# First stage of a hybrid attention and recurrence step: modulation products issued four at a time instead of two

## The chip, the core and the metric

One Trainium2 chip, one of its cores. The time is device microseconds of one execution of the whole program; lower is better. A profile is one execution taken by the hardware profiler; its span runs from the first to the last instruction. The engines are TensorE (PE; its weight loads are PEld), VectorE (DVE), ScalarE (ACT), GpSimd (POOL) and SyncE (SP), which issues all transfers of this kernel from one queue in order.

## What is computed

One layer for 512 tokens of a noisy sample and 128 tokens of context, 2048 features, shared weights. Each group of tokens has its own conditioning vector, from which a large product makes six vectors of shift, scale and gate:

```python
def _adaln(cond, w_mod, b_mod):
    m = jax.nn.silu(cond) @ w_mod + b_mod        # 2048 x 12288
    return jnp.split(m[:, None, :], 6, axis=-1)

sh1, sc1, g1, sh2, sc2, g2 = _adaln(c, p["w_mod"], p["b_mod"])
proj = (x * (1 + sc1) + sh1) @ p["w_in"]
...  # attention and recurrence on parts of proj
x = _post_norm(x, g1, _merge(att, rw, p), p["ln1_g"], p["ln1_b"])
x = _post_norm(x, g2, _swiglu(x * (1 + sc2) + sh2, p), p["ln2_g"], p["ln2_b"])
```

Nothing of the input projection can start on a feature before that feature's shift and scale are there. All is in 32-bit floating point; the large products are made of three products of split operands (high and low part).

## The kernel before

Activations lie transposed: 16 row tiles of 128 features by 640 tokens. The modulation weights are cut into 24 chunks of 512 output columns; chunks 0 to 3 give the shift and 4 to 7 the scale that the input projection needs. These eight are computed first, in the order 0, 4, 1, 5, 2, 6, 3, 7, so that the shift and scale of a group of four row tiles come together (`GROUPS`, L58; `first_mods`, L428). Below, "first chunk" to "eighth chunk" means this order. The other 16 chunks (`wmod_ahead`, L336) come later, with one transfer of 1 MB and four products at a time from a single buffer.

A chunk is 16 products (`wmod_chunk`, L344): the stationary operand is 32 columns of `cs`, the activated conditioning (two columns are real), and the moving operand 512 columns of weights. Product number kt goes to the strip `32 * (kt % 4)` of partitions of the output in PSUM, so four consecutive products use four different strips. After 16 products VectorE copies the result out (`ev`), four tiny products with `sel` add the four strips, and VectorE adds the bias to `mod`. After the second chunk of a group the four row tiles are loaded (`x`), modulated (`h`) and split into a high and a low part (`xh`, `xl`) by VectorE and ScalarE.

`wmod_first` (L326) yields the moving operands of a chunk. Each transfer of 512 KB brings two of the 16 (m = 2); its buffers are `N_W` = 6, shared by tag with later wide tiles. It yields the two products of a transfer and then a number, `W_HOP`.

`first_tiles` (L468) is the first part of the input projection: for each group of four row tiles it does nine output tiles: one (`f` = 0) into the accumulator `ps0`, seven as partial sums in two halves of 320 tokens each (12 products per half, into `m`, then added to `part` by VectorE or copied by ScalarE), and one (`f` = 1) into `ps1`. Their weights are loaded by `load_raw` (L256) in 256 KB transfers into three `raw` buffers and split by ScalarE (`whi`) and VectorE (`wlo`).

What sets TensorE's order is a planner that runs while the program is built (`Jobs`, L126). Each job is a generator. A yielded number says how many microseconds, on the planner's own clock, until that job may go on; the planner always advances the ready job of lowest rank. Ranks: recurrence 0, its side work 1, modulation 2 (`first_mods`, then the other 16 chunks), attention 3, projection 4. A product of 32 columns by 512 costs 0.21 us on this clock. TensorE keeps the order in which the jobs issued; the other engines are ordered by a scheduler, and each instruction waits for its own operands and buffers. When the last group is through its tile `f` = 4, the recurrence begins (`rwkv`, L954): the keys are stored, loaded, squared (`kk`) and reduced by its first product on TensorE.

Of the kernel before, what the change touches and what calls it, by code (L numbers as in the profile page):

```python
# [57 lines left out]
GROUPS = ((0, 4), (4, 4), (8, 4), (12, 4))  # L58
N_PART = 7
TURN = 0.5  # L60
W_HOP = 1.0
M_HOP = 4.9
RANK_R = 0
RANK_S = 1
# [95 lines left out]
def step_kernel(ctx: ExitStack, tc: tile.TileContext, a: dict, o: dict, upto: int = 99, npairs: int = NPAIR, dbg=None):  # L160
# [24 lines left out]
    def rtile(name, n, tag, bufs, dtype=F32):  # L185
        return rp.tile([P, n], dtype, tag=tag, name=nm(name), bufs=bufs)
# [139 lines left out]
    def wmod_first(n, c0, w):  # L326

        m = 1024 // w
        for k in range(0, KT, m):
            raw = rtile("wm", 2 * NT, "w", N_W)[:, :1024].rearrange("p (k c) -> p k c", k=m)  # L330
            DMA.dma_start(out=raw, in_=a["w_mod"][n, k: k + m, :, c0: c0 + w].rearrange("k p c -> p k c"))
            for j in range(m):
                yield raw[:, j]
            yield W_HOP

    def wmod_ahead(n):  # L336
        for k in range(0, KT, 4):
# [90 lines left out]
    def first_mods():  # L428
        for k0, nk in GROUPS:
            n, c0 = divmod(k0 * P, 512)  # L430
            for q in (n, 4 + n):
                yield from wmod_chunk(q, wmod_first(q, c0, nk * P), c0, nk * P)
            for kt in range(k0, k0 + nk):
                x, h = slot("x"), edge("h")
                DMA.dma_start(out=x, in_=a["xT"][kt])
                h1.append(modulate(x, h, hslot, 0, 1, kt))
# [1626 lines left out]
```

## Time and profile before

| | us |
|---|---|
| median of 3 runs (3465.1 to 3469.4) | 3466.15 |
| span of the profiled execution | 3458.1 |
| first products with modulation weights | from 8.2 |
| last of the 128 products of the first eight chunks begins at | 171.6 |
| first product of the recurrence | 231.8 |

The profiled execution's own time is not shown apart from its span; the median stands 8.05 us above it. A row of a timeline gives start, duration, engine, line of the program, operation, tile written and tiles read, columns and sizes, and in brackets how long the engine had been idle and what ended it. One product in 32-bit precision with the modulation weights is recorded as two matmuls, so "x4" are two products and "x8" are four.

### The profile page before, as it was taken

To read this page: it belongs to the slowest core of one execution; us is meant where nothing else is said; L and a number is where in the kernel's file an instruction comes from. 1 tells how busy PE (TensorE), PEld (TensorE's weight loads), DVE (VectorE), ACT (ScalarE), POOL (GpSimd) and SP (SyncE) were. 2 spreads that over 40 slices of the span, in tenths; PEclk is the share of its full clock that TensorE was granted. 3 is DMA by queue.
4 is the path that set the end of the run, shared out by engine and by line. 5 is a ranking of instruction groups with operands and counts; after the bars stand their busy time and mean duration, and the time that the engine had idled before them with its cause. 6 is when DMAs were issued, how large, how long until landed. Compare 5 with 4: busy or idle time off the path is not lost.

```text
span 3458.1 us, 70966 instructions
## 1 busy us (share of the span) xinstructions
PE 3254.0 (94%) x27682; PEld 2972.3 (86%) x27682; DVE 2499.6 (72%) x4478; ACT 1449.3 (42%) x3031; POOL 999.1 (29%) x1034
## 2 busy tenths in 40 slices
PE   7988988999999789999979999999999999999998
PEld 4677766777887678989979999999999999999997
DVE  1356766776776666467688988888887778899677
ACT  1144443443444444445453444444444444333234
POOL 0022222222222122102174544444443332222124
PEclk9999999999999799999989999999999999999998
DMA  8754444444221211076534443444343357888643
GB/s 300 246 177 136 147 145 139 158 157 144 78 62 56 73 31 40 29 252 185 154 110 138 165 130 122 145 134 129 125 142 116 118 186 282 298 285 288 222 140 120
DMA packets 284528, 527.71 MB, mean 153 GB/s; under 512 B 30432, under 2 KB 66720, under 8 KB 284192
## 3 DMA queue, kind: packets, MB, share of 16 engines
q1 hardware_dynamic: 284192, 523.18, 46.1%
q8 instruction: 217, 3.56, 0.4%
q14 instruction: 119, 0.97, 0.1%
HBM read 428.99 MB, written 92.44 MB: 151 GB/s over the span
## 4 chain that ended last, share of the span: by engine, by line
PE 58%; DVE 6%; ACT 2%; issue 2%; DMA 1%; POOL 1%; SPq 0%; ACTq 0%; DVEq 0%; POOLq 0%
PE b L114 50%; PE acc L114 4%; PE m L114 2%; DVE z L228 1%; DVE ql L228 1%; POOL z L228 1%; PE x L114 1%; ACT z L240 0%; PE acc L118 0%; DVE smx L1165 0%; DVE pr L228 0%; ACT P L1166 0%; DVE ip L228 0%; DVE raw L228 0%; DMA raw<-in_w_down_dram 0%
## 5 line engine op out<-in xcount | busy, mean ns | idle before, releaser
L228 DVE TENSOR_TENSOR ql<-raw,qh 128x512 fp32r<-128x512 f32 (+1 forms) x1064 | 887.8, 849 | 260.4 <-ACT qh L1303 247.1
L1303 ACT CAST qh<-raw 128x512 fp32r<-128x512 f32 (+1 forms) x1064 | 633.3, 610 | 830.6 <-PE b L114 647.2
L114 PE MATMUL b<-t,qh 128*128 128x320 f32 x2816 | 622.8, 310 | 8.5 <-ACT qh L1303 7.4
L228 POOL TENSOR_TENSOR raw<-raw,raw 128x512 f32<-128x512 f32 x240 | 354.4, 1477 | 804.4 <-DVE ql L228 546.2
L114 PE MATMUL b<-op,qh 128*128 128x320 f32 x2560 | 553.2, 311 | 1.9 <-ACT qh L1303 1.1
L114 PEld LDWEIGHTS b<-t,qh 128*128 128x128 f32 x2816 | 472.6, 189 | 9.7 <-ACT qh L1303 8.1
L114 PE MATMUL b<-p,qh 128*128 128x320 f32 x2112 | 468.9, 311 | 0.0
L114 PE MATMUL b<-t,ql 128*128 128x320 f32 x1408 | 436.1, 310 | 5.6 <-DVE ql L228 5.5
L114 PEld LDWEIGHTS b<-op,qh 128*128 128x128 f32 x2560 | 425.9, 189 | 4.4 <-ACT qh L1303 2.7
L114 PE MATMUL b<-op,ql 128*128 128x320 f32 x1280 | 379.0, 311 | 5.4 <-DVE ql L228 5.3
L114 PEld LDWEIGHTS b<-p,qh 128*128 128x128 f32 x2112 | 356.0, 189 | 0.3
L114 PE MATMUL b<-p,ql 128*128 128x320 f32 x1056 | 329.0, 312 | 6.9 <-DVE ql L228 6.9
L114 PEld LDWEIGHTS b<-t,ql 128*128 128x128 f32 x1408 | 265.0, 188 | 7.8 <-DVE ql L228 7.7
L114 PEld LDWEIGHTS b<-op,ql 128*128 128x128 f32 x1280 | 236.7, 189 | 8.3 <-DVE ql L228 7.9
L114 PE MATMUL b<-mh,qh 128*128 128x320 f32 x1024 | 230.4, 314 | 6.6 <-ACT qh L1303 6.6
L114 PE MATMUL acc<-xh,whi 128*128 128x320 f32 x928 | 230.3, 330 | 3.5 <-ACT P L1166 2.5
L114 PE MATMUL acc<-xl,whi 128*128 128x320 f32 x928 | 232.9, 333 | 0.0
L114 PE MATMUL acc<-xh,wlo 128*128 128x320 f32 x928 | 231.8, 332 | 0.0
L114 PEld LDWEIGHTS b<-p,ql 128*128 128x128 f32 x1056 | 199.8, 189 | 9.6 <-DVE ql L228 9.6
L228 DVE TENSOR_TENSOR raw<-raw,raw 128x512 f32<-128x512 f32 x240 | 185.4, 780 | 12.5 <-POOL raw L228 9.4
L265 ACT CAST whi<-raw 128x512 fp32r<-128x512 f32 (+1 forms) x156 | 94.9, 609 | 226.4 <-PE acc L114 138.9
L114 PEld LDWEIGHTS b<-mh,qh 128*128 128x128 f32 x1024 | 174.5, 191 | 8.3 <-ACT qh L1303 7.8
(330 smaller groups left out, 5654.5 us busy)
## 6 DMA issues: line engine op xcount, KB each, us to landing
wm<-in_w_mod_dram SPq DMA_DIRECT2D x64, 1024.0 KB, 5.3
raw<-in_w_gate_dram SPq DMA_DIRECT2D x188, 256.0 KB, 2.7
raw<-in_w_up_dram SPq DMA_DIRECT2D x188, 256.0 KB, 2.9
op<-hd SPq DMA_DIRECT2D x136, 320.0 KB, 5.4
raw<-in_w_in_dram SPq DMA_DIRECT2D x132, 256.0 KB, 2.7
wm<-in_w_mod_dram SPq DMA_DIRECT2D x64, 512.0 KB, 6.0
raw<-in_w_out_dram SPq DMA_DIRECT2D x128, 256.0 KB, 3.0
raw<-in_w_down_dram SPq DMA_DIRECT2D x128, 256.0 KB, 5.4
```

The source lines that it names most:

```text
L114: self.eng.matmul(out, lhsT, rhs, start=start, stop=stop)
L228: eng.tensor_tensor(out=out, in0=x, in1=y, op=op)
L265: A.copy(hi, r)
L1303: A.copy(hi, x)
```

## The change

`wmod_first` now starts transfers until it holds four operands, so two transfers of 512 KB; then it yields `W_HOP` first and the four products after it. `W_HOP` goes from 1.0 to 2.4. Transfers, buffers and products are the same ones. The wait of each product for its transfer stays with that product.

```diff
-W_HOP = 1.0
+W_HOP = 2.4
...
     def wmod_first(n, c0, w):
 
         m = 1024 // w
+        held = []
         for k in range(0, KT, m):
             raw = rtile("wm", 2 * NT, "w", N_W)[:, :1024].rearrange("p (k c) -> p k c", k=m)
             DMA.dma_start(out=raw, in_=a["w_mod"][n, k: k + m, :, c0: c0 + w].rearrange("k p c -> p k c"))
-            for j in range(m):
-                yield raw[:, j]
-            yield W_HOP
+            held += [raw[:, j] for j in range(m)]
+            if len(held) >= 4:
+                yield W_HOP
+                yield from held
+                held = []
```

How this moves instructions is seen at three places. The first is TensorE's order in the third chunk (output `x_295`), where the first projection products (`acc_154`, tile `f` = 0) begin. A row "x2" is here two products. Before:

```order
L114 MATMUL x_295<-wm_304,cs 32x512 x2
L114 MATMUL x_295<-wm_308,cs 32x512 x2
L114 MATMUL acc_154<-xh_264,whi_176 128x320 x2
L114 MATMUL acc_154<-xl_265,whi_176 128x320 x2
L114 MATMUL x_295<-wm_322,cs 32x512 x2
L114 MATMUL acc_154<-xh_264,wlo_177 128x320 x2
L114 MATMUL acc_154<-xh_273,whi_176 128x320 x2
L114 MATMUL acc_154<-xl_274,whi_176 128x320 x2
L114 MATMUL acc_154<-xh_273,wlo_177 128x320 x2
L114 MATMUL x_295<-wm_334,cs 32x512 x2
```

And of the change:

```order
L114 MATMUL x_295<-wm_296,cs 32x512 x2
L114 MATMUL x_295<-wm_298,cs 32x512 x2
L114 MATMUL acc_154<-xh_264,whi_176 128x320 x2
L114 MATMUL x_295<-wm_304,cs 32x512 x2
L114 MATMUL x_295<-wm_306,cs 32x512 x2
L114 MATMUL acc_154<-xl_265,whi_176 128x320 x2
L114 MATMUL acc_154<-xh_264,wlo_177 128x320 x2
L114 MATMUL acc_154<-xh_273,whi_176 128x320 x2
L114 MATMUL acc_154<-xl_274,whi_176 128x320 x2
L114 MATMUL acc_154<-xh_273,wlo_177 128x320 x2
```

Where one row of modulation products stood between four projection rows, two now stand between ten. The second place is TensorE's order in the fifth chunk (`x_681`), at the end of the first group of row tiles: `acc_155` is its last tile, `acc_154` the first tile of the second group. Before:

```order
L114 MATMUL x_681<-wm_724,cs 32x512 x2
L114 MATMUL x_681<-wm_728,cs 32x512 x2
L114 MATMUL x_681<-wm_732,cs 32x512 x2
L114 MATMUL x_681<-wm_736,cs 32x512 x2
L114 MATMUL acc_154<-xh_650,whi_686 128x320 x2
L114 MATMUL acc_154<-xl_651,whi_686 128x320 x2
L114 MATMUL x_681<-wm_750,cs 32x512 x2
```

And of the change:

```order
L114 MATMUL acc_155<-xh_291,wlo_606 128x320 x2
L114 MATMUL x_681<-wm_714,cs 32x512 x2
L114 MATMUL x_681<-wm_716,cs 32x512 x2
L114 MATMUL x_681<-wm_728,cs 32x512 x2
L114 MATMUL x_681<-wm_730,cs 32x512 x2
L114 MATMUL acc_154<-xh_650,whi_686 128x320 x2
...
L114 MATMUL acc_154<-xl_669,whi_686 128x320 x2
L114 MATMUL acc_154<-xh_668,wlo_687 128x320 x2
L114 MATMUL x_681<-wm_736,cs 32x512 x2
L114 MATMUL x_681<-wm_738,cs 32x512 x2
```

Two quads follow each other directly there, as four pairs did, and the last one comes nine projection rows later instead of two. The third place is SP's queue for the same transfers (`wm` modulation weights, `raw` projection weights, `x` row tiles). Before:

```order
L435 DMA x_1002<-in_xT_dram 128x640
L331 DMA wm_736<-in_w_mod_dram 128x2x512
L258 DMA raw_791<-in_w_in_dram 128x512
L331 DMA wm_750<-in_w_mod_dram 128x2x512
L435 DMA x_1011<-in_xT_dram 128x640
```

And of the change:

```order
L438 DMA x_1027<-in_xT_dram 128x640
L258 DMA raw_780<-in_w_in_dram 128x512
L438 DMA x_1036<-in_xT_dram 128x640
L438 DMA x_1045<-in_xT_dram 128x640
L332 DMA wm_736<-in_w_mod_dram 128x2x512
L332 DMA wm_738<-in_w_mod_dram 128x2x512
L438 DMA x_1054<-in_xT_dram 128x640
```

The last two modulation transfers of the chunk now stand side by side, behind one projection weight and two row tiles.

## The prediction

> **What bounds the kernel now.** I read the page's busy line first, then the first stage by stretches, then the single rows on TensorE.
>
> ```profile
> span 3458.1 us, 70966 instructions
> PE 3254.0 (94%) x27682; PEld 2972.3 (86%) x27682; DVE 2499.6 (72%) x4478; ACT 1449.3 (42%) x3031; POOL 999.1 (29%) x1034
> ```
>
> TensorE is busy for 94% of the span; nothing else is near it. The change lies in the first 5% or so, so the share of the whole says little. The next view is busy time by stretches, with TensorE's clock, the share of the DMA engines and GB/s at the right.
>
> ```profile
> 20.00:41.00 21.00, 16.19 (x60) 4.57 (x64) 1.88 (x5) 0.00 (x0) 0.00 (x0) 0.70 1.05 389
> 60.00:80.00 20.00, 20.00 (x110) 12.78 (x109) 2.77 (x4) 5.05 (x11) 0.00 (x0) 1.00 0.64 198
> 80.00:100.00 20.00, 18.54 (x109) 11.86 (x108) 8.73 (x17) 6.17 (x11) 0.00 (x0) 1.00 0.82 268
> 100.00:120.00 20.00, 19.86 (x114) 13.61 (x114) 4.90 (x9) 1.85 (x3) 0.00 (x0) 1.00 0.91 329
> 41.00:231.80 190.80, 179.49 (x1068) 128.15 (x1062) 75.06 (x143) 50.33 (x95) 7.91 (x26) 1.00 0.69 227
> ```
>
> The reader is to see two regimes. Up to 41 us the DMA engines are full (share 1.05, 389 GB/s) and TensorE takes each transfer as it lands. From 41 us to 231.8 us, where the recurrence's first product starts, TensorE is busy for 179.5 of 190.8 us at full clock, and the DMA engines for 0.69 of the time. So the first regime is set by bytes, the second by what TensorE must issue. What TensorE waited for between 41 and 200 us is little, and only 1.8 us of it is for a modulation transfer:
>
> ```profile
> PE x L114 <- DMA wm<-in_w_mod_dram: 1.8, 2, 1.5
> PE x L114 <- DVE ev L356: 0.8, 1, 0.8
> PE x L114 <- DVE mod L237: 0.3, 1, 0.3
> PE x L114 <- DVE mod L228: 0.3, 1, 0.3
> ```
>
> **The price of an interruption.** First a pair of modulation products (one row "x4" is two products, each recorded twice) between the half tiles of the input projection, then four of them, which the trace already has from the later chunks:
>
> ```profile
> 66.11 0.30 PE L114 MATMUL m<-xh,wlo 128*128 128x320 f32 x1
> 66.34 1.05 PE L114 MATMUL x<-wm,cs 128*32 128x512 f32 x4
> 67.32 0.41 PE L114 MATMUL m<-xh,whi 128*128 128x320 f32 x1
> 67.57 0.31 PE L114 MATMUL m<-xl,whi 128*128 128x320 f32 x1
> ...
> 69.04 0.31 PE L114 MATMUL m<-xh,wlo 128*128 128x320 f32 x1
> 69.28 1.05 PE L114 MATMUL x<-wm,cs 128*32 128x512 f32 x4
> ```
> ```profile
> 207.41 0.31 PE L114 MATMUL m<-xh,wlo 128*128 128x320 f32 x1
> 207.65 1.07 PE L114 MATMUL x<-wm,cs 128*32 128x512 f32 x8
> 208.64 0.41 PE L114 MATMUL m<-xh,whi 128*128 128x320 f32 x1
> 208.89 0.31 PE L114 MATMUL m<-xl,whi 128*128 128x320 f32 x1
> ```
>
> From pair to pair it is 69.28 - 66.34 = 2.94 us. Between them lie twelve projection products, 0.147 us apart (67.57 to 69.04 is ten steps, 1.47 us), so 1.76 us. The pair therefore costs 2.94 - 1.76 = **1.18 us**. Four products cost the same: 207.41 to 208.89 is 1.48 us, 66.11 to 67.57 is 1.46 us, so **1.20 us**. Four such products stand in four different strips of 32 array columns and run beside one another; two leave half the array empty for the same time.
>
> **The sum.** I count interruptions in the order of TensorE after 44 us, where the first projection product runs; those ahead of it are paced by transfers and stay. A run of pairs with nothing between them counts once per four products. Before: 4 in the third chunk, 8 in the fourth, 6 in the fifth (five runs, one of them of eight products), 8, 8, and 7 (one run of four products): 41. After: 3, 4, 4, 4, 4 and 4: 23, of which two follow another directly. So 41 x 1.18 = 48.4 us goes and 23 x 1.20 = 27.6 us comes: **-20.8 us**. No instruction is added or dropped on any engine apart from a few merges: the same 64 transfers, 128 products, evaluations and modulates.
>
> Does W_HOP's new value move other work? The planner charged two pairs 2 x 0.43 us and now charges a quad 0.85 us, and two half tiles (1.6 us each) fit into a hop of 2.4 us as one did into 1.0 us. At the recurrence's first product, TensorE's order has 12 more projection products ahead of it than before and one modulation quad of the later chunks fewer: 12 x 0.147 - 1.20 = +0.6 us, hidden in the wait that stands there:
>
> ```profile
> 230.92 0.83 ACT L240 ACTIVATE kk<-k,vec 128x640 f32<-128x640 f32 x1 [3.81 <-DMA k<-rkv]
> 231.80 2.29 PE L114 MATMUL m<-cst,kk 128*128 128x2 f32 x10 [5.71 <-ACT kk L240]
> ```
>
> That wait is for a chain of store, load and square, which begins with a projection tile's end and so moves with it; 0.6 us less of 5.71 is left to wait. I count it at 0.
>
> **What the quad waits for.** A matmul waits for its own buffer, not for the quad: if the second transfer is late, two products run and two wait. So ahead of 41 us nothing is lost; rows like the next show a pair at each landing there, 1.36 us apart.
>
> ```profile
> 34.98 1.05 PE L114 MATMUL x<-wm,cs 128*32 128x512 f32 x4 [0.30 <-DMA wm<-in_w_mod_dram]
> 36.34 1.05 PE L114 MATMUL x<-wm,cs 128*32 128x512 f32 x4 [0.30 <-DMA wm<-in_w_mod_dram]
> ```
>
> Later, six buffers are three quads. In the steady part a quad comes every 24 x 0.147 + 1.20 = 4.73 us, so a buffer is refilled 14.2 us ahead of its use (before: six pairs, 17.6 us). What a transfer takes from issue to landing:
>
> ```profile
> L331 SPq DMA_DIRECT2D wm<-in_w_mod_dram x64: 367/368/2007, 2.1 to 157.3; - x64
> ...
> DMA to landing us min/median/max: 3.6/6.0/10.9
> ```
>
> Even the longest, 10.9 us, is inside 14.2. The tight places are where a group of four row tiles ends and quads come close together: in the fifth chunk's last quad and the seventh's. There only twelve projection steps of 0.29 us (two products of 0.147) and two quads lie between a buffer's release and its next use, some 5.6 us, against 6.0 in the median. Before, the same place waited too:
>
> ```profile
> 95.45 1.91 PE L114 MATMUL x<-wm,cs 128*32 128x512 f32 x12
> 98.83 1.05 PE L114 MATMUL x<-wm,cs 128*32 128x512 f32 x4 [1.46 <-DMA wm<-in_w_mod_dram]
> ```
>
> On SP's queue, the fifth chunk's last quad is issued behind a projection weight and two row tiles that wait for VectorE, as its last pair was before. So these places cost from -1.5 us (the wait goes) to 2 x (10.9 - 5.6) = +10.6 us; the nearest row is the wait of 1.46 us that stands there. I take no change.
>
> [...] From 80 to 120 us the rows give (268 + 329)/2 x 40 us = 11.9 MB, 30.7 us at 389 GB/s. TensorE takes 40 us for it now, and 33.5 after, if that stretch has 40/128 of the 20.8 us. [...]
>
> **Sum and time.** 3458.1 - 20.8 = 3437.3 us of span. Around the span lie 3466.15 - 3458.1 = 8.05 us (the median of the runs against the profiled execution, which has no other time shown). That gives **3445 us**, 0.6% less. What a measurement of this kernel can tell from no change is about 0.2%, 7 us.
>
> **The part behind.** The saving has to travel 3200 us. All that follows is tied to the first stage by dependences, so it moves as a block, but its order shifts in phase: in about the first third of TensorE's rows the later modulation quads, the projection and the recurrence stand some ten products earlier or later to each other. Between 231 and 1300 us TensorE's largest waits are on that recurrence (us in total, times, longest):
>
> ```profile
> PE m L114 <- DVE y L228: 22.2, 16, 2.1
> PE m L114 <- DVE tc L601: 17.0, 3, 8.6
> PE m L114 <- DVE nk L228: 9.0, 1, 9.0
> PE m L114 <- POOL sv L847: 8.3, 7, 1.3
> PE m L114 <- DVE t L228: 6.3, 3, 3.7
> PE x L114 <- DVE ev L356: 6.0, 2, 5.7
> ```
>
> They are as likely to shrink as to grow. I keep 10 us either way for them, about the longest single wait (9.0).
>
> **Rivals.**
> - *A new late transfer.* The two tight places wait their 10.6 us: 3445 + 10.6 = 3456 us. For it: share 0.91 at 100 to 120 us. Against: 0.69 in the mean, and a longest wait of 1.5 us. 12%.
> - *Phase behind.* The shifted order catches two more waits of the long kind (9.0 + 8.6 us): 3463 us, within 0.2%. 10%. The opposite, one such wait less, 3436 us: 8%.
> - *Slower: SP's queue is blocked at its head.* Each quad now needs two refills, which SP issues in order behind weights that wait for VectorE. If a quad waits on average longer than 20.8/23 = 0.90 us, the gain is gone. The longest wait of the later quads, which have a single buffer, is the next row:
>
> ```profile
> 201.17 1.07 PE L114 MATMUL x<-wm,cs 128*32 128x512 f32 x8 [2.17 <-DMA wm<-in_w_mod_dram]
> ```
>
>   At 2.17 us for all 23 quads it would be 3445 + 49.9 = 3495 us. Against it: there a refill has one quad's distance, here three. 4%.
> - *It doesn't do what it says.* If the second transfer always lands a pair's length late, each quad splits into two pairs and TensorE idles between: 3466 us. Against it stands the row of 155.70 us, where two pairs in sequence took 1.06 us together. 4%.
>
> ```profile
> 155.70 1.06 PE L114 MATMUL x<-wm,cs 128*32 128x512 f32 x8 [0.26 <-DVE mod L228]
> ```
>
> **Chances and range.** My forecast, 3445 us, has 62%. Faster by over 0.2% (under 3459): 62 + 12 + 8 = 82%. Within: 10 + 4 = 14%. Slower by over 0.2%: 4%. The range goes from 3434 (10 us of luck behind) to 3457 us (the late transfers whole); outside are the long waits of the phase rival, the last two and a little at the low end.
>
> **What would show it.** In the new profile: rows "x8" of 1.07 us from 44 us on, with 24 projection products between them; the fourth chunk's quads 4.7 us apart; "PE x <- DMA wm" still under 4 us from 41 to 200 us; the recurrence's first product at 231.8 - 20.8 = 211 us; the same distance from it to the end, to 10 us. The forecast is wrong if quads run as two rows "x4" with a wait between, if the DMA share reaches 1 between 80 and 120 us, or if the first product comes at 211 us and the end doesn't move with it.

## The result, and the profile after

| | before | after |
|---|---|---|
| median of five runs each, us | 3466.15 (3465.1 to 3474.04) | 3446.62 (3442.77 to 3457.02) |
| ratio, 95% interval | | 0.9944 [0.9929, 0.9960] |
| span of the profiled execution, us | 3458.1 | 3441.0 |
| first product of the recurrence, us | 231.8 | 206.5 |

The change is faster by 0.56%, 19.5 us. The profiled execution of after took 3442.77 us with a span of 3441.0, so 1.8 us lie around a span. The one of before must then have taken some 3459.9 us: it stands below all five of that kernel's times in the table. (The change adds three lines, so line numbers behind L329 are three higher.)

The page of after, the span and the busy line (busy time and share of the span, number of instructions):

```profile
span 3441.0 us, 70942 instructions
PE 3231.1 (94%) x27682; PEld 2967.5 (86%) x27682; DVE 2504.2 (73%) x4478; ACT 1449.0 (42%) x3031; POOL 1000.9 (29%) x1034
```

TensorE is busy for 3231.1 us against 3254.0, 22.9 less with the same 27682 instructions. Its idle time went up from 204.1 to 209.9 us. So TensorE saved what was forecast, and 5.8 us of it came back as waits. What happened in the first stage, its stretches show (busy time of PE, PEld, DVE, ACT, POOL; then the granted TensorE clock, the DMA share, GB/s):

```profile
20.00:41.00 21.00, 15.06 (x60) 4.41 (x60) 2.07 (x5) 0.00 (x0) 0.00 (x0) 0.76 1.05 389
60.00:80.00 20.00, 20.00 (x141) 15.88 (x139) 3.37 (x5) 5.91 (x13) 0.00 (x0) 1.00 0.70 226
80.00:100.00 20.00, 17.74 (x117) 12.81 (x117) 9.53 (x19) 4.99 (x8) 0.00 (x0) 1.00 1.00 362
100.00:120.00 20.00, 20.00 (x139) 15.99 (x137) 7.46 (x14) 3.10 (x5) 0.00 (x0) 1.00 0.81 282
41.00:206.48 165.48, 157.80 (x1072) 127.40 (x1064) 77.01 (x145) 51.29 (x97) 7.57 (x26) 0.99 0.76 254
```

Ahead of 41 us nothing moved. From 41 us to the recurrence's first product the stretch is 165.48 us instead of 190.80: 25.3 us shorter, 21.7 of them busy time. TensorE's idle time in it fell from 11.3 to 7.7 us, so the waits that came back lie behind it. The rate of work is best seen at 60 to 80 us: 141 matmul records in the same 20 us, against 110. The DMA engines, which pass 389 GB/s at 20 to 41 us, are full between 80 and 100 us (share 1.00, 362 GB/s).

TensorE's timeline of after, at the places that the prediction named (start, duration; in brackets the idle time and what ended it):

```profile
66.89 1.06 PE L114 MATMUL x<-wm,cs 128*32 128x512 f32 x8
...
71.60 1.06 PE L114 MATMUL x<-wm,cs 128*32 128x512 f32 x8
...
93.66 1.05 PE L114 MATMUL x<-wm,cs 128*32 128x512 f32 x4 [1.45 <-DMA wm<-in_w_mod_dram]
94.98 1.05 PE L114 MATMUL x<-wm,cs 128*32 128x512 f32 x4 [0.27 <-DMA wm<-in_w_mod_dram]
...
206.48 1.28 PE L114 MATMUL m<-cst,kk 128*128 128x2 f32 x10 [3.11 <-ACT kk L240]
```

Quads stand 71.60 - 66.89 = 4.71 us apart and take 1.06 us each. The fifth chunk's last quad, at 93.66 us, is the one that waits, and it shows what a wait does to a quad: it falls apart into two pairs of 1.05 us, so its transfer costs the idle time and one more set. TensorE's waits between 41 and 200 us in after (us in total, times, longest):

```profile
PE x L114 <- DMA wm<-in_w_mod_dram: 3.7, 3, 2.0
PE acc L114 <- DVE xl L228: 0.5, 1, 0.5
```

Of the 3.7 us, 2.0 belong to one of the later quads with a single buffer, which waited 2.17 us before. So the first stage did what the change says. The rest of the story lies behind it.

### The profile page after: what moved, and what is told of

Same layout as the page of the kernel before. It is cut to its first block, busy times and chain, and to the rows that moved or that the text cites. A ratio compares the mean times of both kernels' runs of the same rounds, so it can differ in the third digit from the quotient of the medians.

```text
span 3441.0 us, 70942 instructions
## 1 busy us (share of the span) xinstructions
PE 3231.1 (94%) x27682; PEld 2967.5 (86%) x27682; DVE 2504.2 (73%) x4478; ACT 1449.0 (42%) x3031; POOL 1000.9 (29%) x1034
## 4 chain that ended last, share of the span: by engine, by line
PE 59%; DVE 7%; ACT 2%; issue 2%; DMA 1%; POOL 1%; SPq 0%; ACTq 0%; DVEq 0%; POOLq 0%
PE b L114 50%; PE acc L114 5%; PE m L114 3%; DVE z L228 1%; DVE ql L228 1%; POOL z L228 1%; PE x L114 1%; DVE pr L228 0%; ACT z L240 0%; DMA raw<-in_w_down_dram 0%; DVE ip L228 0%; PE acc L118 0%; DVE smx L1168 0%; DVE z L237 0%; DVE raw L228 0%
```

## Experiments

Two numbers describe each kernel, counted in TensorE's order. **Sets**: a run of n modulation products with nothing between them, from the first projection product on (about 44 us), counts n/4 rounded up. **Pace**: how many projection products stand ahead of the last set of the eight chunks; few means that the chunks go through quickly. `W_HOP` does not cost time by itself: it is the least time on the planner's clock between two sets, so it sets the pace. (Where an expectation below says "charged", it means these waits added up.)

### What does a set cost?

Theory: products in different strips run side by side, and a set of one to four costs one product's time. Rival: each interruption of the projection has a price of its own, whatever is in it. Four kernels change the size of the set, or put all products of a set into one strip.

Sets of one, from the kernel before:

```diff
-W_HOP = 1.0
+W_HOP = 0.4
...
             for j in range(m):
                 yield raw[:, j]
-            yield W_HOP
+                yield W_HOP
```

> One product at a time (hop 0.4): 72 sets of at most four instead of 41. 'Strips side by side': each set costs 1.18 us, however few strips it fills: +31 x 1.18 = 37 us against before; first product of the recurrence near 268 us, time near 3503. Rival 'a product costs its own share' (half a pair): first product at 232 us, time 3466.

Sets of eight, from the changed kernel:

```diff
-W_HOP = 2.4
+W_HOP = 4.8
...
-            if len(held) >= 4:
+            if len(held) >= 8:
```

> Eight products at a time (four transfers, hop 4.8): 11 interruptions instead of 21, but 22 sets of four products instead of 23. 'Strips side by side': eight cost two sets, so the price of the products stays (22 x 1.0) and only the re-entry, some 0.2 us, is saved ten times; four of six buffers are asked for at once, so waits for transfers grow by about that or more: first product of the recurrence 204 to 212 us, time 3442 to 3452. Rival 'fixed price': ten interruptions of 1.2 us less, first product near 194 us, time 3435.

All products of a set in one strip, once in the changed kernel and once in the kernel before (`strip=1` for the eight chunks only; the sums are the same, since the four strips are added afterwards):

```diff
-            g = kt % 4
-            T.matmul(ps[32 * g: 32 * g + 32, :w], cs[:, 2 * kt: 2 * kt + 32], raw, start=kt < 4, stop=kt >= 12)
+            g, i = (kt % 4, kt // 4) if strip is None else (kt // 4, kt % 4)
+            T.matmul(ps[32 * g: 32 * g + 32, :w], cs[:, 2 * kt: 2 * kt + 32], raw, start=i == 0, stop=i == 3)
```

> Quads in the same order, but the four products of a quad go to one strip of 32 columns instead of four. Theory 'strips side by side' (four products cost what one costs because they stand in four strips): each then runs behind the other, about 0.87 us each, a quad 3.5 to 3.8 us instead of 1.2; 23 quads give some 55 to 60 us, and the pairs ahead of 41 us take 1.74 us instead of one landing of 1.36, some 6 us; first product of the recurrence near 270 us, time about 3510 us. Rival 'fixed price of an interruption' (leaving and re-entering the projection costs 1.2 us whatever stands in it): 3447 us, nothing changes.

> The kernel before, but both products of a pair go to one strip. 'Strips side by side': a pair costs 1.74 + 0.2 instead of 1.18, 41 times 0.8 and 6 us ahead of 41 us: about 3505 us, and within some 5 us of the quads on one strip, since now only the sum of products counts. Rival 'fixed price': 3466 us, 20 us above the quads on one strip.

One set in each, from TensorE's timelines. Singles:

```profile
68.36 1.04 PE L114 MATMUL x<-wm,cs 128*32 128x512 f32 x2
```

Octets:

```profile
64.22 1.92 PE L114 MATMUL x<-wm,cs 128*32 128x512 f32 x16
```

A pair in one strip, then a quad in one strip:

```profile
73.66 1.90 PE L114 MATMUL x<-wm,cs 128*32 128x512 f32 x4
```
```profile
76.07 3.62 PE L114 MATMUL x<-wm,cs 128*32 128x512 f32 x8
```

One, two and four products in different strips take 1.04, 1.05 and 1.07 us; eight, two to a strip, 1.92. In one strip two take 1.90 and four 3.62. So what counts is the largest number of products in any one strip, 1.04 us for the first and 0.86 for each further one (1.04 + 3 x 0.86 = 3.62); three more strips cost 0.02 to 0.03 us. In the traces of before and after the start of each further strip lies 6 to 7 ns behind that of the one before.

The totals follow. Singles: 3514.7 us, ratio 1.0142 [1.0123, 1.0160], with 72 sets; 31 more than before are 31 x 1.18 = 37 us, and 50 were measured. In the profiled executions the recurrence's first product comes 34.0 us later (265.82 us), near what the sets give; 11.5 us lie behind it. (The pace of the singles is 640, against 492 before.) Quads in one strip: 3494.1 us, 1.0083 [1.0070, 1.0097]. Pairs in one strip: 3497.1 us, 1.0090 [1.0074, 1.0105]. These are 16 and 8 us below the times expected. With no strips beside one another, going from pairs to quads is worth 3.0 us in the total and 8.8 us at the recurrence's first product (273.28 to 264.50), where the real change gained 25.3. Of the 8.8, 2.7 are a shorter wait for `kk` (5.63 to 2.93 us). The rival, a fixed price for an interruption, falls: 40 interruptions became 21 in both cases.

Octets came to 3439.4 us, 0.9929 [0.9916, 0.9941], faster than the change. But they have 22 sets, nearly as many as the quads' 23, and reach the recurrence later than the quads (211.36 against 206.48 us). So something other than the sets is at work.

### The same program again

> The changed kernel again, beside the others of this chip. Both theories: ratio to before 0.994 to 0.996, first product of the recurrence near 206 us.

The changed kernel itself: 3452.2 us, ratio 0.9958 [0.9945, 0.9972], the recurrence's first product at 208.04 us. The stage repeats to 1.6 us. The total is 5.5 us higher; between the medians lie 11 us where the first comparison had 19.5. The mean granted clock of the profiled executions was 0.965 here and 0.969 there.

### Is it W_HOP?

The change does two things: it makes sets of four, and it raises `W_HOP` from 1.0 to 2.4. Each alone:

```diff
-W_HOP = 1.0
+W_HOP = 2.4
```

> The kernel before with W_HOP 2.4 alone. If the gain is from the set of four: 37 sets instead of 41 (some pairs now stand in a row), -4.7 us, but the modulation falls behind the projection, and TensorE waits for the modulated row tiles at the end of each group: 3 times 3 to 5 us more. First product of the recurrence 231 to 242 us, time 3463 to 3478. Rival 'the planner's new number brings the gain': first product near 206 us, time near 3447.

```diff
-W_HOP = 2.4
+W_HOP = 1.0
```

> The change with W_HOP left at 1.0. 21 sets instead of 23 (-2.4 us), but the modulation runs ahead of the projection as fast as the planner allows, with 288 instead of 540 projection products ahead of the last quad, so quads wait for transfers: at least 6 us more of it than the 3.7 us of the change. First product of the recurrence 208 to 222 us, time 3447 to 3462. Rival 'only the grouping counts': like the change, 206 us and 3446.

Pairs with 2.4: 3478.8 us, 1.0042 [1.0029, 1.0055], slower than before by 14 us, although it has 37 sets where before had 41. Of the 9 to 15 us that TensorE was to wait for row tiles, 3.9 show between 41 us and the recurrence (2.3 for `xh`, 1.6 for `xl`), and the recurrence begins at 232.6 us, close to before; so most of the 14 us lie behind it. Quads with 1.0: 3449.9 us, 0.9959 [0.9946, 0.9973], but by another way than expected. The recurrence begins at 234.88 us, later than in the kernel before. TensorE's timeline of the quads with 1.0, at the place where four of its nine waits for modulation transfers stand together:

```profile
99.92 1.05 PE L114 MATMUL x<-wm,cs 128*32 128x512 f32 x4 [0.72 <-DMA wm<-in_w_mod_dram]
101.15 1.05 PE L114 MATMUL x<-wm,cs 128*32 128x512 f32 x4 [0.18 <-DMA wm<-in_w_mod_dram]
103.13 1.05 PE L114 MATMUL x<-wm,cs 128*32 128x512 f32 x4 [0.93 <-DMA wm<-in_w_mod_dram]
104.49 1.05 PE L114 MATMUL x<-wm,cs 128*32 128x512 f32 x4 [0.30 <-DMA wm<-in_w_mod_dram]
```

In the steady part a quad comes after every half tile, and the transfers just keep up: the stretch from 41 to 100 us has a DMA share of 0.98, and most quads there are still one row "x8" of 1.07 us. At 100 us they fall behind, and the two quads shown fall into two pairs each, with a wait ahead of each pair. That is the prediction's rival "it doesn't do what it says", at this place and not throughout. The second row is the stretch up to the recurrence:

```profile
41.00:100.00 59.00, 57.96 (x378) 38.71 (x372) 21.27 (x42) 16.41 (x31) 0.00 (x0) 0.98 0.98 351
41.00:234.88 193.88, 175.65 (x1117) 131.97 (x1109) 78.42 (x146) 50.50 (x95) 7.50 (x26) 0.95 0.73 251
```

Against the change's 165.48 us it is 28.4 us longer. TensorE idles 18.2 us instead of 7.7, with 9.5 instead of 3.7 us of waits for modulation transfers and 7.0 instead of 3.1 for `kk`. It is busy for 17.9 us more: six more quads of the later chunks stand ahead of the recurrence (168 products against 144), some 7.2 us, and the granted clock is 0.95 instead of 0.99. Yet the time is only 3 us from the change's, so the late start was made up behind it, some 7.2 us of it by work that was merely moved ahead. That again points to the part behind.

### Pace, with the sets kept

The octets once more, and quads with two further numbers:

> The octets of the run before, unchanged: 22 sets, the first recurrence product at 211.4 us there, 3439.4 us. If sets of eight are truly faster than sets of four: 3436 to 3445 us again, and at least 8 us below the quads of this call with their other planner numbers (both stages of sets being equal, the gain would have to lie in the order behind). If what set them apart was the order and the granted clock behind the stage: anything from 3438 to 3458, with the mean granted clock going down as the time goes up.

```diff
-W_HOP = 2.4
+W_HOP = 2.0
```

> The changed kernel with W_HOP 2.0 in place of 2.4: 21 interruptions and 22 sets in place of 21 and 23, so the stage costs the same within one set of 1.2 us, and the wm waits of TensorE stay below 5 us between 41 and 200 us. Theory (sets set the gain; the rest is the order and the clock of the part behind): 3442 to 3458 us, 0.2 to 0.7% below the kernel before. Rival (the planner's number itself carries the gain): a shift of over 15 us against the change's 3446.6 to 3452.2.

```diff
-W_HOP = 2.4
+W_HOP = 3.2
```

> The changed kernel with W_HOP 3.2 in place of 2.4: 23 sets in 23 interruptions, the same number of sets. Theory (sets set the gain): 3442 to 3458 us. Rival (the planner's number carries it, as with pairs at 2.4, which were 14 us slower than pairs at 1.2): 3460 us or more.

Octets: 3439.2 us again, 0.9920 [0.9905, 0.9935]. Quads with 2.0: **3430.3 us**, 0.9900 [0.9885, 0.9916], the fastest of all kernels here. Quads with 3.2: 3457.3 us, 0.9977 [0.9967, 0.9988]. With 22, 22 and 23 sets the three lie 27 us apart. My theory, that the sets set the gain and the rest is scatter within 3442 to 3458 us, missed the quads with 2.0 by 12 us, where the rival asked for a shift of over 15 us and 16 to 22 came; octets are not better than quads as such. (With 2.0 the waits for modulation transfers were 5.3 us, where less than 5 was expected.) The executions of one program lie up to 14 us apart (3442.8 to 3457.0 us for the change), but those of the quads with 2.0 and with 3.2 don't overlap: 3429.5 to 3438.2 against 3453.6 to 3465.8 us. So the planner's number moves the time by itself, and the kernel before needs to be compared at equal pace. Two pairs kernels for that:

```diff
-W_HOP = 1.0
+W_HOP = 1.3
```

> The kernel before with W_HOP 1.3 in place of 1.0: 39 interruptions charged 50.7 in all, where the change's 21 are charged 50.4, and 41 sets. It is the change's twin in the planner's sum, with pairs in place of quads. Theory (a set saves about 1.2 us wherever it is placed, and the planner's number moves the order behind by itself): 41 - 23 = 18 sets, 21 us above the change's 3446.6 to 3452.2, so 3463 to 3478 us. Rival (the order behind, set by the charged sum, carried the gain): within 8 us of the change, 3440 to 3460 us.

```diff
-W_HOP = 1.0
+W_HOP = 0.5
```

> The kernel before with W_HOP 0.5 in place of 1.0: 36 interruptions charged 18 in all, where the quads at 1.0 have 20 charged 20, and 38 sets where they have 21. Theory: 17 sets more, 20 us above those quads' 3449.9, so 3462 to 3478 us. Rival (the charged sum sets the order and that sets the time): within 8 us of them, 3442 to 3458 us.

Pairs with 1.3: 3477.8 us, 1.0046 [1.0033, 1.0059], as the theory had it. Pairs with 0.5: 3446.6 us, 0.9948 [0.9934, 0.9961], as the rival had it: **the kernel before with one number changed and no quads at all gains as much as the change.** All kernels with strips side by side, by pace:

| kernel | pace | sets | modulation products ahead of the recurrence | first recurrence product, us | from first to last transposed block, us | median, us |
|---|---|---|---|---|---|---|
| pairs, 0.5 | 420 | 38 | 160 | 229.6 | 1017.1 | 3446.6 |
| pairs, 1.0 (before) | 492 | 41 | 148 | 231.8 | 1039.6 | 3465 |
| pairs, 1.3 | 564 | 41 | 144 | 232.7 | 1061.7 | 3477.8 |
| pairs, 2.4 | 648 | 37 | 140 | 232.6 | 1057.5 | 3478.8 |
| quads, 1.0 | 288 | 21 | 168 | 234.9 | 1020.8 | 3449.9 |
| quads, 2.0 | 480 | 22 | 152 | 212.3 | 1029.3 | 3430.3 |
| quads, 2.4 (the change, twice) | 540 | 23 | 144 | 206.5, 208.0 | 1049.1, 1054.3 | 3446.6, 3452.2 |
| quads, 3.2 | 648 | 23 | 140 | 215.9 | 1053.1 | 3457.3 |
| octets, 4.8 (twice) | 516 | 22 | 148 | 211.4, 211.3 | 1038.9, 1035.4 | 3439.4, 3439.2 |

The sixth column takes the recurrence's 16 block transposes on VectorE as milestones (one for each half step) and gives the time from the first to the last. From the last one to the end it is 2138.5 to 2146.8 us in every kernel, so little of this happens there. These columns come from one profiled execution each: that of pairs with 0.5 stands 3.2 us below its median, that of pairs with 1.3 7.0 us above.

Three rows of pairs have quads of nearly equal pace. Against them the quads gain, at the first recurrence product without the wait for `kk` that stands there, 19.0 us (492 and 480), 21.3 and 19.3 us (564 and 540) and 17.9 us (648 and 648). Their sets are 19, 18 and 14 fewer, at 1.2 us: 22.8, 21.6 and 16.8 us. That is the prediction's sum, to within 4 us. In the total they gain 35, 26 to 31, and 22 us, so at nearly equal pace the part behind isn't equal either.

Down each group of the table the part behind gets longer with a later pace and then stays: for pairs from 1017.1 to some 1060 us, for quads from 1020.8 to some 1050. The octets, at 516, stand between the quads of 480 and 540. The rows for it are the stretches from the first to the last milestone, and, second, between the fourteenth and the fifteenth. Pairs with 0.5:

```profile
280.98:1298.09 1017.11, 930.40 (x11926) 758.03 (x11927) 715.92 (x1590) 459.60 (x1179) 248.70 (x412) 0.95 0.35 110
1146.32:1223.09 76.77, 66.16 (x789) 55.02 (x790) 58.48 (x128) 37.43 (x91) 19.35 (x29) 0.94 0.13 35
```

The kernel before:

```profile
274.42:1314.00 1039.58, 935.00 (x11916) 759.61 (x11914) 713.13 (x1586) 456.24 (x1175) 249.22 (x406) 0.95 0.34 110
1147.90:1237.73 89.83, 66.89 (x739) 55.15 (x738) 60.93 (x131) 34.78 (x83) 17.71 (x27) 0.79 0.11 32
```

Pairs with 1.3:

```profile
278.13:1339.79 1061.66, 954.45 (x11922) 775.13 (x11922) 717.24 (x1587) 456.15 (x1174) 244.83 (x406) 0.93 0.34 109
1171.93:1263.19 91.26, 70.69 (x773) 57.83 (x772) 65.06 (x138) 37.40 (x90) 17.49 (x27) 0.80 0.16 45
```

After:

```profile
250.46:1299.61 1049.15, 942.10 (x11941) 765.11 (x11942) 718.59 (x1589) 456.21 (x1176) 248.76 (x407) 0.94 0.34 110
1138.32:1222.07 83.75, 67.83 (x740) 56.33 (x740) 60.20 (x129) 34.40 (x82) 17.49 (x27) 0.82 0.13 34
```

TensorE runs the same number of matmuls to within 0.2%, but they keep it busy for 930 to 954 us, at granted clocks from 0.95 down to 0.93, and what it waits is 87 us with 0.5 (1017.11 - 930.40) against 105 to 107 us in the other three. One interval alone, the second row, is 13 us longer in the kernel before than with 0.5, at a clock of 0.79 instead of 0.94.

One kernel speaks against pace as the whole cause. Quads in one strip have the pace of the change, 540, and nearly the same order on TensorE, but a slower first stage. Their stretch is 8.7 us shorter than the change's, at nearly the same busy time:

```profile
309.17:1349.59 1040.42, 943.34 (x11941) 766.57 (x11942) 717.29 (x1589) 456.20 (x1176) 250.12 (x407) 0.94 0.34 111
```

Pairs in one strip take 1040.7 us there, at the pace of the kernel before. So the link to the pace is shown among the kernels of the table only; whether the time at which the first stage ends matters too was not tested. The single wait that differs most between the kernel before and pairs with 0.5 is for `tc`, in the recurrence's chain on VectorE. Pairs with 0.5, from the first to the last milestone:

```profile
PE m L114 <- DVE y L228: 25.2, 15, 2.5
PE m L114 <- ACT mrb L816: 13.4, 9, 4.8
...
PE m L114 <- DVE tc L601: 6.8, 3, 5.4
```

It is 6.8 us here, 17.0 in the kernel before and 10.7 in the quads with 2.0. (The wait for `mrb` goes the other way, 13.4 against 4.5.) The longest wait for `tc` in the kernel before, and the same product with 0.5:

```profile
1171.52 1.29 PE L114 MATMUL m<-tc,mab 32*32 32x32 f32 x80 [8.57 <-DVE tc L601]
```
```profile
1164.55 0.28 PE L114 MATMUL acc<-wlo,ch 128*128 128x256 f32 x1
1165.58 0.94 PE L114 MATMUL m<-tc,mab 32*32 32x32 f32 x80 [0.76 <-DVE tc L601]
```

With 0.5, products of the attention (`acc` from `ch`) stand ahead of it, and TensorE waits 0.76 instead of 8.57 us. So at this place a quicker pace leaves TensorE other work that it can do. That the number alone moves the part behind is shown. Why a quicker pace helps over the whole of it is not: neither the work that fills the gaps nor the clock was changed by itself, and one may follow from the other.

## Why the prediction was right, and where it was not

- **What bounds the stage: right.** Between 41 us and the recurrence the time went down with TensorE's busy time, 21.7 of 25.3 us, while the DMA share rose from 0.69 to 0.76.
- **The price of a set, 1.18 and 1.20 us: right,** and it is a price for a strip's product, as singles, octets and the one-strip kernels show. Quads were to be 4.73 us apart and are 4.71.
- **The sum of -20.8 us: right for the stage.** The first recurrence product came at 206.5 us instead of 211. Without the `kk` wait the stage gained 22.7 us. At nearly equal pace the runs give 18 to 21 us for 14 to 19 sets.
- **"I count it at 0", the `kk` wait: 2.6 us off.** It went from 5.71 to 3.11 us, so the start of the recurrence moved by more than the sets. Among the kernels it is anything from 2.64 to 9.53 us.
- **Transfers at two tight places, taken at 0: right to some 1.5 us.** The fifth chunk's quad waits 1.45 + 0.27 us, where before a wait of 1.46 us stood, and falls apart, which is one set of 1.2 us more; the seventh's does not wait at all. The sign that was to show the forecast wrong, a DMA share of 1 between 80 and 120 us, came (1.00 at 80 to 100) and cost no more than that; in the quads with 1.0, at 0.98 from 41 to 100 us, TensorE's waits grew only from 100 us on. The first stretch again shows 389 GB/s, the rate with which the prediction reckoned the bytes of 80 to 120 us.
- **"Does W_HOP's new value move other work?": the step that failed.** The prediction found twelve projection products more ahead of the recurrence, priced them at 0.6 us, and let them vanish in a wait. But `W_HOP` had moved the pace from 492 to 540, and the runs show that this number alone moves the part behind. For pairs, 492 to 564 costs 12.8 us in the total; by that slope the change's step costs 12.8 x 48/72 = 8.5 us (an estimate, which the kernels with one strip don't bear out). Measured from the first recurrence product to the end, after is 3441.0 - 206.5 = 3234.5 us against 3226.3: 8.2 us longer, and 13.9 in the second execution. The prediction allowed 10 us either way, "as likely to shrink as to grow". The size was about right, but the sign was left open and could have been looked for by changing the number.
- **8.05 us around the span: wrong,** it is 1.8. The rest was the low time of the execution that the profile of before had caught. Taken as a difference to the median it did no harm: the span came out 3.7 us above the 3437.3 forecast, and the median 1.6 us above 3445.

So the time was met by a stage that gained 4.5 us more than forecast and a part behind that gave 8.2 us back. That the two partly cancelled is luck; the mechanism of the first stage is not. What the change could have brought near the old pace is seen in the quads with 2.0: 35 us.

## What to carry to other kernels

Where the stationary operand has 32 columns, as here, count sets by the products in the fullest strip, not by instructions: three more strips were nearly free (1.04 to 1.07 us). And a change that brings along a new number for a planner is two changes; run the old code with some other numbers first, since here one number moved the time by 32 us (3446.6 to 3478.8 with pairs), more than the edit under test. Compare the two versions at equal pace, and then tune the number again.

## What the hardware showed that was not expected

In the recurrence part the granted clock differs with the order of the work: over the interval shown above it is 0.79 in the kernel before and 0.94 with 0.5. Ten microseconds of the kernel before, inside that interval, then the first 6 us behind the wait for `tc` of 8.57 us:

```profile
1167.90:1177.90 10.00, 6.38 (x152) 5.11 (x156) 4.02 (x8) 1.61 (x4) 0.46 (x2) 0.50 0.01 2
1171.52:1177.52 6.00, 6.00 (x123) 4.72 (x127) 0.49 (x1) 1.23 (x3) 0.00 (x0) 0.50 0.01 3
```

And with 0.5, behind the wait of 0.76 us:

```profile
1165.58:1171.58 6.00, 5.20 (x180) 4.11 (x180) 2.58 (x5) 3.50 (x6) 0.00 (x0) 1.00 0.25 57
```

After the long wait TensorE works without a break (6.00 of 6.00 us), but at half clock (0.50); after the short one the clock is full (1.00). In the kernel before, the clock falls inside the long wait and is full again only some 8 us behind it:

```profile
1163.00:1165.70 2.70, 0.00 (x0) 0.00 (x0) 2.70 (x5) 0.83 (x1) 0.00 (x0) 1.00 0.00 0
1165.80:1171.50 5.70, 0.00 (x0) 0.00 (x0) 5.46 (x8) 0.00 (x0) 0.46 (x2) 0.50 0.00 0
1177.52:1179.40 1.88, 1.88 (x72) 1.82 (x63) 1.57 (x3) 0.66 (x2) 0.00 (x0) 0.50 0.04 9
1179.50:1186.20 6.70, 3.07 (x55) 2.49 (x53) 6.58 (x14) 5.18 (x11) 0.00 (x0) 1.00 0.00 0
```

So if the wait is what brings the half clock, it is paid twice, once as idle time and once in the slow products behind it (1.29 us for the 80 recorded matmuls with `tc`, against 0.94). That may be why the interval's 67 us of busy time come out nearly equal at clocks of 0.79 and 0.94 although the second did 50 matmuls more. It is my reading of these two places: no run here changed the clock alone.
